# A hybrid RG-LRU and neighbourhood-attention layer: how silu(c) is spread, which loads come in halves, where h is split, and when the bias tables and the decay are made

## The chip, the cores and the metric

The kernel runs on one core of one Trainium2 chip. The metric is the device time of one execution in microseconds. Three runs of the kernel before gave 560.02, 560.91 and 561.32 us, so the median is 560.91 us. One more execution was recorded by the hardware profiler; it took 561.25 us.

## The reference, cut to what matters

One encoder layer, batch 1, 512 tokens, 1024 channels, all in float32. `c` is one vector of 1024 numbers. It gives a scale and a shift for each channel, the normalised input is multiplied and shifted by them to `h`, and `h` goes through one wide projection whose eight parts feed a recurrent branch and an attention branch.

```python
mod = jax.nn.silu(c) @ w_c[l] + b_c[l]
shift, scl, gate = jnp.split(mod, 3, axis=-1)
h = rms_norm(x, g_pre[l]) * (1.0 + scl[:, None, :]) + shift[:, None, :]
proj = h @ w_in[l]
xa, za, q, k, v, zb, ga, gb = jnp.split(proj, split_pts, axis=-1)
...
h_fwd = rg_lru(xa, w_r_f[l], b_r_f[l], w_i_f[l], b_i_f[l], lam_f[l], reverse=False)
h_bwd = rg_lru(xa, w_r_b[l], b_r_b[l], w_i_b[l], b_i_b[l], lam_b[l], reverse=True)
y_a = ((h_fwd + h_bwd).astype(x.dtype) * jax.nn.silu(za)) @ w_pa[l]
y_b = (neighbourhood_attention(qh, kh, vh, rpb[l]) * jax.nn.silu(zb)) @ w_pb[l]
merged = jax.nn.sigmoid(ga) * y_a + jax.nn.sigmoid(gb) * y_b
x = x + gate[:, None, :] * (merged @ w_o[l])
return rms_norm(x, g_final)
```

In `rg_lru` each channel has a decay, `exp(-8 r softplus(-lam))`; in the attention `rpb` is a table of 16 heads x 15 x 31 biases that is added to the scores.

## The kernel before, in words

**Arithmetic.** Each large product is computed as three products on TensorE: both factors are split into a high part of reduced precision (fp32r) and a low part, and high x high, high x low and low x high are added in PSUM (`mm3`). ScalarE makes the high part by a cast, VectorE or GpSimd the low part by a subtraction. So most matrices appear in pairs: `hx` and `lx` (x times the scale), `vh` and `vl` (the weights of v), `hh` and `hl` (h), `whi` and `wlo` (weights of a projection).

**The head of the program.** `par` is one array of 128 x 128 parameters; its first eight rows are `c`. The kernel loads those eight rows as `c8`, computes silu(c) times two there, and spreads it over all 128 partitions by eight matmuls with eight rows each (L460): the result is `pair`, two banks of PSUM that hold the 1024 values on every partition. VectorE multiplies each 128 x 1024 block `wc` of the modulation weights with `pair` and sums (L540; for the first scale in two halves, L536). Each such sum is the scale or the shift of 128 channels (`sc`, `shc`). TensorE meanwhile repeats a matmul of ones (`fill`, L513).

**v first.** v is computed from x times the scale, since the row norm can be applied at the end (`vout`). There are eight units of v (two column halves by four row tiles), each a sum over eight steps k of three matmuls: 192 matmuls. Five units go along step by step, as x and the weights arrive; the other three follow when a step is there.

**h.** When the row norms are known they are spread by TensorE (L506) and copied to `rbs`. For each of the eight blocks k, GpSimd multiplies x with `rbs` into an SBUF tile `ht` (L559), ScalarE applies scale and shift in place (L560) and casts the result to `hh` (L405), and VectorE subtracts for `hl` (L408). The projections (`proj`, matmuls into `acc`, 24 for each) need all eight pairs.

**The rest.** Four groups of attention come first, two pairs of heads each: six projections for q, k and z, then scores (`sp`), softmax, transposes (`pt`) and products with v (`pv`). `bias` makes the tables of one pair of heads on GpSimd, six instructions into three tiles `nb` (L685). Then come the recurrent branch, whose decay constants `small` computes by about thirty instructions of 128 x 16 or 128 x 32 on VectorE (L469, L884 to L902), the merge, the output projection and the final norm.

**Order.** `Plan` is a list scheduler that runs on the host when the program is built. Every operation has a rank, an estimated cost, and the tiles it reads and writes; the planner places operation after operation on the engine on which one can start soonest, prefers the lower rank among those that start at about the same time, and so writes the whole instruction stream of each engine. `HEAD` is a table of ranks that replaces the written ones for some 170 operations of the head. Engines execute their streams in order, and all loads are issued by the SP queue in the order of its stream. `lock=True` tells the planner that a VectorE operation and GpSimd keep each other out. PSUM has eight banks; `LIMITS` bounds how many a class of tiles may hold.

Of the kernel before, what the change touches and what calls it, by code (L numbers as in the profile page):

```python
# [1292 lines left out]
```

## Time and profile before

| | |
|---|---|
| median of three runs | 560.91 us (560.02 to 561.32) |
| profiled execution | 561.25 us, of which the span from the first to the last instruction is 559.3 us |
| TensorE matmul busy | 546.6 us, 98% of the span, 2725 records |
| VectorE, ScalarE, GpSimd busy | 410.5, 329.7 and 127.9 us |
| mean granted TensorE clock | 0.993 |
| moved by DMA | 89.37 MB, mean 160 GB/s; about 410 GB/s in the first 50 us |
| chain that ended last | TensorE 92%, VectorE 5%, DMA 2% |

The 1.95 us between the profiled time and the span lie before the first and behind the last instruction. A row of the groups names a line, an engine, an operation and its tiles, then its count, the busy time and the mean duration of one; behind the next bar stands the time that the engine sat idle just before. A row of the timeline begins with the start of the first instruction and the time from there to the end of the last one that it merges; the idle time before it stands at its end in brackets, with what ended it. Matmuls overlap: a row of one 128x512 matmul reads 0.39 us, though the next one starts about 0.23 us later. A 128x128 matmul in float32 leaves two records.

### The profile page before, as it was taken

The page shows a single profiled execution, that of the slowest core. Times are in us where ns is not written, and L with a number is a line of the kernel's source. Part 1 is how long each engine was busy: PE and PEld are TensorE (multiplying, and loading weights), DVE is VectorE, ACT ScalarE, POOL GpSimd, SP SyncE. Part 2 cuts the span into 40 slices and gives each one's busy share as a digit, 9 for nine tenths or more (in the row PEclk, how much of TensorE's full clock was granted, in tenths as well). Part 3 has the DMA queues.
Part 4 walks back from the last instruction along what each step waited for, and adds up shares of the span by engine and source line. Part 5 has one row for each costly group of instructions (what it writes and reads, how often), then busy time and mean ns, then how long its engine had stood idle before and what let it go on. Part 6 is the DMA issues. An engine that isn't in the chain of part 4 may idle for free.

```text
span 559.3 us, 7626 instructions
## 1 busy us (share of the span) xinstructions
PE 546.6 (98%) x2725; PEld 455.1 (81%) x2725; DVE 410.5 (73%) x715; ACT 329.7 (59%) x575; POOL 127.9 (23%) x114
## 2 busy tenths in 40 slices
PE   8899979999999999999999999999999999999995
PEld 8688768888888888888887888788788888888885
DVE  4978994787787688898458958876967973469523
ACT  4576732763773673675996994996698242223243
POOL 0638865456556540000000000000000000000220
PEclk8999989999999999999999999999999999999999
DMA  8999890544544545125145044221329422380002
GB/s 345 408 410 404 320 361 17 150 150 175 147 161 185 134 152 208 39 95 190 43 132 184 0 151 133 75 102 52 110 86 364 145 83 76 138 313 1 1 38 113
DMA packets 31837, 89.37 MB, mean 160 GB/s; under 512 B 4784, under 2 KB 5944, under 8 KB 31800
## 3 DMA queue, kind: packets, MB, share of 16 engines
q1 hardware_dynamic: 31496, 88.56, 45.0%
q8 instruction: 21, 0.34, 0.3%
q10 hardware_dynamic: 304, 0.33, 0.2%
q14 instruction: 16, 0.13, 0.1%
HBM read 82.42 MB, written 6.46 MB: 159 GB/s over the span
## 4 chain that ended last, share of the span: by engine, by line
PE 92%; DVE 5%; DMA 2%; issue 1%; ACT 1%; ACTq 0%
PE acc L411 77%; PE hx L411 5%; PE pv L411 3%; PE pt L811 2%; PE sp L411 2%; PE gt L411 2%; DVE hhl L408 1%; DMA wraw<-in_w_in_dram 1%; DVE wc L540 1%; DVE vhl L408 1%; DVE xhl L550 1%; DMA c<-in_par_dram 1%; PE pair L460 0%; PE mi L506 0%; DVE va L629 0%
## 5 line engine op out<-in xcount | busy, mean ns | idle before, releaser
L411 PE MATMUL acc<-hhl,whi 128*128 128x512 f32 x784 | 244.4, 392 | 3.1 <-DVE hhl L408 3.1
L411 PEld LDWEIGHTS acc<-hhl,whi 128*128 128x128 f32 x784 | 146.8, 189 | 34.2 <-DVE hhl L408 4.3
L411 PE MATMUL acc<-hhl,wlo 128*128 128x512 f32 x392 | 153.3, 391 | 0.0
L411 PEld LDWEIGHTS acc<-hhl,wlo 128*128 128x128 f32 x392 | 73.9, 189 | 15.6
L1158 POOL TENSOR_TENSOR yo<-yo,gfin 128x512 f32<-128x512 f32 x6 | 8.1, 1358 | 338.6 <-ACT xr L1155 338.6
L405 ACT CAST whi<-wraw 128x1024 fp32r<-128x1024 f32 x72 | 74.1, 1044 | 1.0 <-PE acc L411 0.8
L408 POOL TENSOR_TENSOR wlo<-wraw,whi 128x1024 fp32r<-128x1024 f32 x23 | 56.5, 2462 | 62.7 <-ACT whi L405 32.8
L408 DVE TENSOR_TENSOR wlo<-wraw,whi 128x1024 fp32r<-128x1024 f32 x49 | 59.2, 1219 | 3.1 <-ACT whi L405 2.8
L411 PE MATMUL acc<-woh,mhl 128*128 128x512 f32 (+1 forms) x144 | 40.4, 365 | 0.0
L411 PE MATMUL acc<-yahl,whi 128*128 128x512 f32 x128 | 39.4, 389 | 0.0
L411 PE MATMUL acc<-ybhl,whi 128*128 128x512 f32 x128 | 39.4, 389 | 0.0
L1043 DVE SCALAR_TENSOR_TENSOR gm<-gm,acc 128x512 f32<-128x512 f32 x16 | 11.0, 687 | 33.0 <-PE acc L411 33.0
L800 ACT ACTIVATE p<-p,mn 128x192 f32<-128x192 f32 (+1 forms) x64 | 30.4, 477 | 6.7 <-DVE mn L793 6.6
L685 POOL TENSOR_TENSOR nb<-msk,braw 128x192 f32<-128x192 f32 (+1 forms) x48 | 34.1, 745 | 0.0
L793 DVE CUSTOM_DVE_ANT_0 p<-sp,nb 128x192 f32<-128x192 f32 (+1 forms) x64 | 30.8, 604 | 0.3
L411 PEld LDWEIGHTS acc<-woh,mhl 128*128 128x128 f32 x144 | 26.1, 189 | 4.4
L949 DVE SCALAR_TENSOR_TENSOR xc<-acc,prm,xc 128x511 f32<-128x511 f32 (+1 forms) x24 | 18.0, 750 | 14.8 <-ACT xc L942 14.1
L411 PEld LDWEIGHTS acc<-ybhl,whi 128*128 128x128 f32 x128 | 24.0, 188 | 5.0
L411 PEld LDWEIGHTS acc<-yahl,whi 128*128 128x128 f32 x128 | 24.0, 188 | 5.0
L411 PE MATMUL acc<-wol,mhl 128*128 128x512 f32 (+1 forms) x72 | 26.3, 365 | 0.0
L411 PE MATMUL hx<-vhl,xhl 128*128 128x512 f32 x96 | 24.8, 399 | 1.4 <-DVE vhl L408 1.4
L411 PE MATMUL acc<-ybhl,wlo 128*128 128x512 f32 x64 | 24.9, 389 | 0.0
(186 smaller groups left out, 990.9 us busy)
## 6 DMA issues: line engine op xcount, KB each, us to landing
wraw<-in_w_in_dram SPq DMA_DIRECT2D x56, 512.0 KB
wc<-in_w_m_dram SPq DMA_DIRECT2D x24, 512.0 KB
vt<-vscr SPq DMA_DIRECT2D x20, 256.0 KB
wv<-in_w_v_dram SPq DMA_DIRECT2D x8, 512.0 KB
vscr<-va SPq DMA_DIRECT2D x8, 512.0 KB
wvt<-in_w_vt_dram SPq DMA_DIRECT2D x8, 512.0 KB
wraw<-in_w_pb_dram SPq DMA_DIRECT2D x8, 512.0 KB
wraw<-in_w_pa_dram SPq DMA_DIRECT2D x8, 512.0 KB
```

Source lines behind the costliest of these rows:

```text
L405: return lambda e: nc.scalar.copy(o(), i()) if e == "ACT" else nc.vector.tensor_copy(o(), i())
L408: return lambda e: ENGINE[e].tensor_tensor(o(), a(), b().bitcast(F32), op=ALU.subtract)
L411: nc.tensor.matmul(o, a, b, start=first, stop=last)
L540: op("DVE", dve(1024) + 0.08, lambda e: nc.vector.tensor_tensor_reduce(out=t.ap, in0=t.ap, in1=pair, scale=g, scalar=b, op0=ALU.mult, op1= ...
L550: op("DVE", dve(512) + 0.06, lambda e: nc.vector.scalar_tensor_tensor(lx[k].ap, xk(), scs[k].ap, hx[k].ap.bitcast(F32), op0=ALU.mult, op1= ...
L685: nc.gpsimd.tensor_tensor(o, mv, view, op=ALU.subtract)
L793: nc.vector.tensor_tensor_reduce(out=o, in0=v(spv(h, e)[:, :nk]), in1=v(nb[:, h, :nk]), scale=1.0, scalar=3e38, op0=ALU.add, op1=ALU.min, ...
L800: nc.scalar.activation(pv2(i), pv2(i), AF.Exp, bias=mn.ap[:, c:c + 1], scale=-1.0, accum_out=sm.ap[:, 4 * h + b:4 * h + b + 1])
L811: nc.tensor.transpose(ptp.ap[:, j * P:(j + 1) * P], pt_.ap[:, j * P:(j + 1) * P], ident.ap)
L949: nc.vector.scalar_tensor_tensor(a, b, wcol, a, op0=ALU.mult, op1=ALU.add)
L1043: op("DVE", dve(512), lambda e: nc.vector.scalar_tensor_tensor(t.ap, t.ap, 1.0, o.ap, op0=ALU.add, op1=ALU.mult), n - 1.9, r=[o], rw=[t], ...
L1158: op(("DVE", "POOL"), (dve(w), pool_(w)), lambda e: ENGINE[e].tensor_tensor(y(), y(), gfin[n].ap[:, gs], op=ALU.mult), rank + 0.1, r=[gfin ...
```

## The change

The matmul that spreads silu(c) now contracts over 128 rows: `c8` is cleared by VectorE and its first eight rows are written. There is one load of `par` in place of two. The spread is computed twice: first into two plain banks `cb0`, of which the first scale reads each half by itself, and then into `pair` for all others. The first block of x and the first block of v's weights come in two loads of 256 KB each. The sixth unit of v goes along with the five, one step behind. h is written by ScalarE into a PSUM tile (class `hs`, two banks at most), from which the high part is cast and the low part subtracted. The bias tables of the first pair of heads are asked for behind the tenth projection and later, and the decay behind the thirtieth. The table `HEAD` has new numbers throughout, which moves loads and instructions of the head.

```diff
-LIMITS = {"cb": 2, "hx": 6, "acc": 3, "sp": 8, "pt": 2, "pv": 2, "mi": 2, "hd": 3, "gt": 8}
+LIMITS = {"cb": 2, "hx": 6, "acc": 3, "sp": 8, "pt": 2, "pv": 2, "mi": 2, "hs": 2, "gt": 8}
...
-    "rn": -24.5555, "sq3": -24.3814, "rd": -24.3812, "sq1": -24.3808, "rbs": -23.8168, "sq0": -23.8167,
+    "rb": -26.6107, "rd": -25.5608, "rv": -25.1307, "rn": -25.1305, "sq0": -24.9778, "sq2": -24.9777,
...
-    tan8, c8 = const("tan8", [8, P]), const("c8", [8, P])
+    tan8, c8 = const("tan8", [8, P]), const("c8", [P, P])
-    op("ACT", 0.45, lambda e: nc.scalar.dma_start(c8.ap, par[:8, :]), -41, w=[c8], late=2.6, name="c8")
-    op("ACT", 0.45, lambda e: nc.scalar.dma_start(par_sb.ap, par), -40, w=[par_sb], late=3.3, name="par")
+    clear = op("DVE", 0.25, lambda e: nc.vector.memset(c8.ap, 0.0), -40, w=[c8])
+    op("ACT", 0.45, lambda e: nc.scalar.dma_start(par_sb.ap, par), -40, w=[par_sb], late=2.1)
...
-    cbs = [B("cb") for _ in range(2)]
+    def spread_c(t, n, rank, name):
+        def f(e):
+            for k in range(4):
+                nc.tensor.matmul(t.ap[:, k * P:(k + 1) * P], ident.ap[:, 4 * n + k:4 * n + k + 1].to_broadcast([P, P]), c8.ap,
+                                 start=True, stop=True)
+        op("PE", 0.9, f, rank, r=[ident, c8], w=[t], name=name)
+    cb0 = [B("mi") for _ in range(2)]
     for n in range(2):
-        def f(e, n=n):
-            for k in range(4):
-                nc.tensor.matmul(cbs[n].ap[:, k * P:(k + 1) * P], ident.ap[:8, 4 * n + k:4 * n + k + 1].to_broadcast([8, P]), c8.ap,
-                                 start=True, stop=True)
-        op("PE", 0.6, f, -21 + n, r=[ident, c8], w=[cbs[n]], name=f"cb{n}")
+        spread_c(cb0[n], n, -21 + 0.1 * n, f"ca{n}")
+    cbs = [pl.tile("cb", lambda i, n=n: bank(i, "cb", n)) for n in range(2)]
+    for n in range(2):
+        spread_c(cbs[n], n, -20.5 + 0.1 * n, f"cb{n}")
...
-    for j in range(4):
+    xs = [xT[0].part(0, S), xT[0].part(S, D)] + [xT[k // 2] for k in range(2, KD)]
+    for j in range(2):
+        load(xs[j], whole(xs[j]), x_t[0, :, j * S:j * S + S], -19.9 + 0.1 * j, 262144, spare=2, name=f"x0{'ab'[j]}")
+    for j in range(1, 4):
         load(xT[j], whole(xT[j]), x_t[j], -19.9 + 0.1 * j, 524288, spare=2, name=f"x{j}")
...
         hh[k], hl[k] = two("hhl") if k else (T("hh", F32R), T("hl", F32R))
-        t = T("ht")
+        t, b = T("ht"), B("hs")
...
-        op("ACT", act(512, 2), lambda e: nc.scalar.activation(t.ap, t.ap, AF.Identity, scale=scs[k].ap, bias=shs[k].ap), k - 1.195,
-           r=[scs[k], shs[k]], rw=[t], name=f"hs{k}")
-        op("ACT", act(512), cast(whole(hh[k]), whole(t)), k - 1.19, r=[t], w=[hh[k]], name=f"hh{k}")
-        op("DVE", dve(512), sub(whole(hl[k]), whole(t), whole(hh[k])), k - 1.18, r=[t, hh[k]], w=[hl[k]], lock=True, wait=1.45, name=f"hl{k}")
+        op("ACT", act(512, 2), lambda e: nc.scalar.activation(b.ap, t.ap, AF.Identity, scale=scs[k].ap, bias=shs[k].ap), k - 1.195,
+           r=[t, scs[k], shs[k]], w=[b], name=f"hs{k}")
+        op("ACT", act(512), cast(whole(hh[k]), whole(b)), k - 1.19, r=[b], w=[hh[k]], name=f"hh{k}")
+        op("DVE", dve(512), sub(whole(hl[k]), whole(b), whole(hh[k])), k - 1.18, r=[b, hh[k]], w=[hl[k]], name=f"hl{k}")
...
+        for n in range(2 * (k == 0)):
+            load(src[n], whole(src[n]), w_v[k, :, z[n]], k - 4.5, 262144, spare=2, name=f"wv0{'ab'[n]}")
...
-    for m, u in enumerate(VU[5:]):
+        vmm(VU[5], k, [0, 1, 2], k + 0.9 if k < KD - 1 else k + 0.5)
+    for m, u in enumerate(VU[6:]):
...
-    small(9, [main[8]])
...
-            nbs.append(bias(pr, n0 + BD * (1 - pr % 2), gate_of(n0, 2) if pr else [main[6]]))
+            if pr:
+                nbs.append(bias(pr, n0 + BD * (1 - pr % 2), gate_of(n0, 2)))
...
+            if not pr:
+                nbs.append(bias(pr, n0 + 4, [main[10]]))
...
+    small(31, [main[30]])
```

Three places show how the instructions move. The first is TensorE at the start of the program (`hx` with `onesc` are the fills, `mi` with `par_sb` is a transpose of the parameters, `c` with `ident` is the spread of silu(c), and `vhl` with `xhl` is the first matmul of v). Before:

```order
L513 MATMUL hx_129<-onesc 128x128 x8
L441 MATMUL mi_150<-ident,par_sb 128x128
L460 MATMUL pair<-c_79,ident 128x128 x8
L513 MATMUL hx_129<-onesc 128x128 x10
L411 MATMUL hx_194<-vhl_183,xhl_177 128x512
```

And now:

```order
L523 MATMUL hx_128<-onesc 128x128 x4
L441 MATMUL mi_139<-ident,par_sb 128x128
L523 MATMUL hx_128<-onesc 128x128 x2
L460 MATMUL mi_152<-c_79,ident 128x128 x4
L460 MATMUL mi_159<-c_79,ident 128x128 x4
L460 MATMUL pair<-c_79,ident 128x128 x8
L523 MATMUL hx_128<-onesc 128x128 x2
L411 MATMUL hx_194<-vhl_176,xhl_184 128x512
```

Four fills instead of eight stand ahead of the transpose, the spread has sixteen matmuls instead of eight, and two fills instead of ten stand between it and v.

The second place is GpSimd where h is made (`ht` is x times the row norm, `wlo` the low part of a projection's weights, `nb` a bias table, `vt` a cleared half tile). Before:

```order
L559 TENSOR_TENSOR ht_632<-xT_188,rbs_508 128x512
L408 TENSOR_TENSOR wlo_662<-wraw_461,whi_634 128x1024
L685 TENSOR_TENSOR nb_695<-msk,braw_517 128x256 x2
L685 TENSOR_TENSOR nb_716<-msk,braw_517 128x192 x2
L685 TENSOR_TENSOR nb_737<-msk,braw_517 128x192 x2
L708 MEMSET vt_683 64x512
L708 MEMSET vt_697 64x512
L408 TENSOR_TENSOR wlo_777<-wraw_588,whi_699 128x1024
L685 TENSOR_TENSOR nb_802<-msk,braw_651 128x256 x2
L685 TENSOR_TENSOR nb_823<-msk,braw_651 128x192 x2
L685 TENSOR_TENSOR nb_841<-msk,braw_651 128x192 x2
```

And now:

```order
L569 TENSOR_TENSOR ht_701<-xT_178,rbs_525 128x512
L408 TENSOR_TENSOR wlo_715<-wraw_592,whi_698 128x1024
L723 MEMSET vt_692 64x512
L723 MEMSET vt_706 64x512
L408 TENSOR_TENSOR wlo_766<-wraw_613,whi_752 128x1024
L700 TENSOR_TENSOR nb_787<-msk,braw_660 128x256 x2
L700 TENSOR_TENSOR nb_803<-msk,braw_660 128x192 x2
L700 TENSOR_TENSOR nb_816<-msk,braw_660 128x192 x2
L408 TENSOR_TENSOR wlo_826<-wraw_637,whi_773 128x1024
L700 TENSOR_TENSOR nb_842<-msk,braw_668 128x256 x2
L700 TENSOR_TENSOR nb_856<-msk,braw_668 128x192 x2
L700 TENSOR_TENSOR nb_873<-msk,braw_668 128x192 x2
```

The two sets of bias tables stand one `wlo` later each; all of `ht` and one more `wlo` come before them.

The third place is VectorE where the last blocks of h are split (`hhl` is a tile with a high and a low part, `lt` and `hb` belong to the decay). Before:

```order
L712 STREAM_TRANSPOSE sht_721<-shc 128x32
L408 TENSOR_TENSOR hhl_671<-ht_590,hhl_671 128x512
L408 TENSOR_TENSOR hhl_732<-ht_538,hhl_732 128x512
L469 SCALAR_TENSOR_TENSOR lt_84<-prm 128x16
L884 TENSOR_SCALAR hb<-prm 128x32
L890 TENSOR_SCALAR lt_86<-lt_85 128x16
```

And now:

```order
L727 STREAM_TRANSPOSE sht_708<-shc 128x32
L408 TENSOR_TENSOR hhl_720<-hs_690,hhl_720 128x512
L408 TENSOR_TENSOR hhl_723<-hs_710,hhl_723 128x512
L408 TENSOR_TENSOR hhl_746<-hs_739,hhl_746 128x512
L408 TENSOR_TENSOR ql_789<-acc_633,qh_780 128x512
L754 SCALAR_TENSOR_TENSOR kl_795<-acc_656,kh_785 128x512
```

The subtractions read `hs`, a PSUM tile, instead of `ht`, and the decay is gone from here; its instructions now stand in front of the low part of the fourth group's second k.

More of the change, by code (lines that the diff above doesn't have):

```diff
@@ L37 @@
 VP, VG = 4, 3
-LIMITS = {"cb": 2, "hx": 6, "acc": 3, "sp": 8, "pt": 2, "pv": 2, "mi": 2, "hd": 3, "gt": 8}
+LIMITS = {"cb": 2, "hx": 6, "acc": 3, "sp": 8, "pt": 2, "pv": 2, "mi": 2, "hs": 2, "gt": 8}
 BLOCKS = [(0, 24, 8), (8, 32, 0), (24, 32, 0), (40, 24, 0)]
 HEAD = {
[26 rows of a table removed]
-    "decay": 29.4012
[27 rows of a table added]
 }
@@ L374, in layer, with bank @@
     rest, twin, plain = [], [], set()
-    def bank(i, cls):
+    def bank(i, cls, half=0):
         if cls == "cb":
@@ L379, in bank @@
             twin.append(i)
-            return pair[:, 512 * len(twin) - 512:512 * len(twin)]
+            return pair[:, 512 * half:512 * half + 512]
         if i not in twin:
@@ L536, in modulate @@
                 op("DVE", dve(512) + 0.08, lambda e, j=j, z=z: nc.vector.tensor_tensor_reduce(
-                    out=t.ap[:, z], in0=t.ap[:, z], in1=cbs[j].ap, scale=g, scalar=a.ap if j else b, op0=ALU.mult, op1=ALU.add,
-                    accum_out=r.ap if j else a.ap), -0.5, r=[cbs[j], mods, prm] + [a] * j, rw=[t], w=[r if j else a], name=f"mod{k}{m}{j}")
+                    out=t.ap[:, z], in0=t.ap[:, z], in1=cb0[j].ap, scale=g, scalar=a.ap if j else b, op0=ALU.mult, op1=ALU.add,
+                    accum_out=r.ap if j else a.ap), -0.5, r=[cb0[j], mods, prm] + [a] * j, rw=[t], w=[r if j else a], name=f"mod{k}{m}{j}")
             return
@@ L548, in split_x @@
         op("ACT", act(512, 1), lambda e: nc.scalar.activation(hx[k].ap, xk(), AF.Copy, scale=scs[k].ap), k - 1.19,
[L549 removed]
+           r=[xs[k], scs[k]], w=[hx[k]], name=f"hx{k}")
         op("DVE", dve(512) + 0.06, lambda e: nc.vector.scalar_tensor_tensor(
             lx[k].ap, xk(), scs[k].ap, hx[k].ap.bitcast(F32), op0=ALU.mult, op1=ALU.subtract), k - 1.18,
[L552 removed]
+           r=[xs[k], hx[k], scs[k]], w=[lx[k]], lock=True, name=f"lx{k}")
@@ L554, in make_h @@
     def make_h(k):
         hh[k], hl[k] = two("hhl") if k else (T("hh", F32R), T("hl", F32R))
-        t = T("ht")
+        t, b = T("ht"), B("hs")
         xk = lambda: xT[k // 2].ap[:, k % 2 * 512:k % 2 * 512 + 512]
-        op("POOL", pool_(512), lambda e: nc.gpsimd.tensor_tensor(t.ap, xk(), rbs.ap, op=ALU.mult), k - 1.2, r=[xT[k // 2], rbs], w=[t], name=f"ht{k}")
-        op("ACT", act(512, 2), lambda e: nc.scalar.activation(t.ap, t.ap, AF.Identity, scale=scs[k].ap, bias=shs[k].ap), k - 1.195,
-           r=[scs[k], shs[k]], rw=[t], name=f"hs{k}")
@@ L562, in make_h @@
-        op("ACT", act(512), cast(whole(hh[k]), whole(t)), k - 1.19, r=[t], w=[hh[k]], name=f"hh{k}")
-        op("DVE", dve(512), sub(whole(hl[k]), whole(t), whole(hh[k])), k - 1.18, r=[t, hh[k]], w=[hl[k]], lock=True, wait=1.45, name=f"hl{k}")
+        op("POOL", pool_(512), lambda e: nc.gpsimd.tensor_tensor(t.ap, xk(), rbs.ap, op=ALU.mult), k - 1.2, r=[xs[k], rbs], w=[t], name=f"ht{k}")
+        op("ACT", act(512, 2), lambda e: nc.scalar.activation(b.ap, t.ap, AF.Identity, scale=scs[k].ap, bias=shs[k].ap), k - 1.195,
+           r=[t, scs[k], shs[k]], w=[b], name=f"hs{k}")
@@ L565, in split_v @@
+        op("ACT", act(512), cast(whole(hh[k]), whole(b)), k - 1.19, r=[b], w=[hh[k]], name=f"hh{k}")
+        op("DVE", dve(512), sub(whole(hl[k]), whole(b), whole(hh[k])), k - 1.18, r=[b, hh[k]], w=[hl[k]], name=f"hl{k}")
     def split_v(k):
         t, z = W("wv"), (slice(0, S), slice(S, D))
-        load(t, whole(t), w_v[k], k - 4.5, 524288, spare=2, name=f"wv{k}")
+        src = [t] * 2 if k else [t.part(0, S), t.part(S, D)]
+        if k:
+            load(t, whole(t), w_v[k], k - 4.5, 524288, spare=2, name=f"wv{k}")
@@ L571, in split_v @@
             vh[k, n], vl[k, n] = (hi, whole(hi)), (lo, whole(lo))
-            op("ACT", act(512), lambda e, hi=hi, n=n: nc.scalar.copy(hi.ap, t.ap[:, z[n]]), k - 1.1, r=[t], w=[hi], name=f"vh{k}{n}")
-            op(*(("POOL", pool_(512)) if k and n else (("DVE", "POOL"), (dve(512), pool_(512)))), sub(whole(lo), lambda n=n: t.ap[:, z[n]], whole(hi)), k - 1.09, r=[t, hi],
+            op("ACT", act(512), lambda e, hi=hi, n=n: nc.scalar.copy(hi.ap, t.ap[:, z[n]]), k - 1.1, r=[src[n]], w=[hi], name=f"vh{k}{n}")
+            op(*(("POOL", pool_(512)) if k and n else (("DVE", "POOL"), (dve(512), pool_(512)))), sub(whole(lo), lambda n=n: t.ap[:, z[n]], whole(hi)), k - 1.09, r=[src[n], hi],
                w=[lo], lock=True, name=f"vl{k}{n}")
@@ L903, in small @@
         for j in range(0, len(steps), 2):
-            op("DVE", 0.4, lambda e, j=j: [f() for f in steps[j:j + 2]], rank, r=[lt[1], prm], rw=[lt[2]], w=[sp2, sp4],
-               name="decay")
-    small(9, [main[8]])
+            op("DVE", 0.4, lambda e, j=j: [f() for f in steps[j:j + 2]], rank + 8, r=[lt[1], prm], rw=[lt[2]], w=[sp2, sp4],
+               lock=True, name="decay")
     LO_A = ("POOL",)
```

8 lines of the change are left out of this document (3 added, 5 removed), and 51 rows, old and new, of the table HEAD.

## The prediction

> **What bounds the kernel now.** I read the busy times by stage first, then what TensorE waited for, then the timelines of the stages that are not full, and the chain of waits last. The stages here are: up to the first matmul of v, v up to the first projection, the projections up to the first scores, everything up to the last matmul, and the tail. The columns are each engine's busy time and records, the granted clock, DMA.
>
> ```profile
> 0.00:10.98 10.98, 9.27 (x53) 8.91 (x54) 3.51 (x11) 4.92 (x8) 1.02 (x10) 0.89 0.84 325
> 10.98:58.00 47.02, 45.58 (x202) 37.14 (x202) 41.55 (x63) 31.62 (x52) 26.99 (x21) 0.99 1.03 408
> 58.00:96.29 38.29, 35.16 (x147) 27.76 (x145) 29.29 (x47) 15.69 (x22) 28.88 (x27) 0.96 0.65 233
> 96.29:552.90 456.61, 456.57 (x2329) 381.31 (x2328) 333.80 (x589) 276.48 (x493) 70.97 (x57) 1.00 0.37 124
> 552.90:559.30 6.40, 0.00 (x0) 0.00 (x0) 2.31 (x8) 1.02 (x2) 0.00 (x0) 0.90 0.36 140
> PE acc L411 <- DVE hhl L408: 3.1, 1, 3.1
> PE hx L411 <- DVE vhl L408: 1.4, 1, 1.4
> ```
>
> From 96.29 us on, TensorE is busy for 456.57 of 456.61 us at full clock, so that whole part moves with its beginning. Only the first 96 us can be shortened, and there the long waits are one of 3.1 and one of 1.4 us.
>
> The pace comes from the next rows: four 128x512 matmuls from 22.20 to 23.11 us are 0.2275 us each.
>
> ```profile
> 22.20 1.07 PE L411 MATMUL hx<-vhl,xhl 128*128 128x512 f32 x4
> 23.11 0.39 PE L411 MATMUL hx<-vh,xhl 128*128 128x512 f32 x1
> 43.48 1.05 PE L506 MATMUL mi<-ident,rxc 128*128 128x128 f32 x8
> 44.28 0.94 PE L411 MATMUL hx<-vhl,xhl 128*128 128x512 f32 x3
> 69.42 0.39 PE L411 MATMUL acc<-hhl,whi 128*128 128x512 f32 x1
> 72.91 0.50 PE L411 MATMUL acc<-hhl,whi 128*128 128x512 f32 x1 [3.10 <-DVE hhl L408]
> ```
>
> The 192 matmuls of v need 43.68 us and the spread of the norms 0.80 us, 44.48 together; the stage took 47.02, an excess of **2.54 us**. The six projections (144 matmuls) need 32.76 us; their stage took 38.29, an excess of **5.53 us**. Of that, 69.42 to 72.91 less one matmul is 3.26 us.
>
> The clock, in stretches of 3.4 us as it was granted:
>
> ```profile
> 5.03:8.45 3.42, 3.23 (x27) 1.00 1.01 407
> 8.45:11.86 3.41, 3.41 (x17) 0.50 1.03 417
> 22.10:25.51 3.41, 1.97 (x10) 1.00 1.02 407
> 69.70:73.10 3.40, 0.29 (x2) 1.00 1.02 277
> 73.10:76.50 3.40, 3.40 (x9) 0.53 0.99 392
> ```
>
> An almost empty stretch (0.29 us busy) is followed by one at half speed: 3.4 us of matmuls do the work of 1.7, so the wait of 3.26 cost about 1.7 more. But a stretch with 3.23 us busy also led to half speed at 8.45. What was odd in it is the spread of silu(c): eight rows instead of 128. A stretch with 1.97 us of full matmuls kept full speed.
>
> **The change, part by part.** *h from PSUM, tables and decay later.* The cause of the wait of 3.26 us:
>
> ```profile
> 65.96 2.41 POOL L408 TENSOR_TENSOR wlo<-wraw,whi 128x1024 fp32r<-128x1024 f32 x1
> 68.33 3.38 POOL L685 TENSOR_TENSOR nb<-msk,braw 128x256 f32<-128x256 f32 x6
> 66.75 6.11 DVE L408 TENSOR_TENSOR hhl<-ht,hhl 128x512 fp32r<-128x512 f32 x2
> 61.01 0.86 DVE L629 SCALAR_TENSOR_TENSOR va<-hx,rxc,va 128x256 fp32r<-128x256 f32 x2
> 60.49 4.34 POOL L685 TENSOR_TENSOR nb<-msk,braw 128x256 f32<-128x256 f32 x6
> L408 DVE TENSOR_TENSOR hhl<-ht,hhl 128x512 fp32r<-128x512 f32 x6 | 11.2, 1895 | 0.8 <-ACT hhl L405 0.8
> L408 DVE TENSOR_TENSOR ql<-acc,qh 128x512 fp32r<-128x512 f32 x2 | 1.4, 684 | 0.0
> L560 ACT ACTIVATE ht<-ht,shc,sc 128x512 f32<-128x512 f32 x8 | 6.5, 815 | 4.8 <-DVE shc L540 3.7 <-POOL ht L559 1.1
> ```
>
> Two subtractions from SBUF took 6.11 us: they stood until GpSimd had ended a `wlo` and six `nb`. Six of them average 1895 ns. At 61.01 two operations with a PSUM source ran in 0.86 us while GpSimd worked on `nb`: they are not held. `ql`, the same subtraction from PSUM, takes 684 ns. So the eight low parts cost 0.68 each, VectorE gets back 6 x (1.895 - 0.684) = 7.3 us, and the wait goes: the excess of **5.53** is removed, with the half-speed stretch. No row has ScalarE writing to PSUM in this shape; between the copy out of PSUM (0.59 us for `rbs`) and twice the 0.815 of L560, I take 0.815, the same operation. ScalarE is busy for 15.69 of 38.29 us in the stage, which covers 8 x 0.8 more; without that cover it would be 6.5 us. [...]
>
> What is late next? GpSimd now does eight `ht`, five `wlo`, two memsets and twelve `nb` in a row. By these rows (`ht` 10.09 for eight, `wlo` 2.41, memsets 1.10, `nb` 4.34 + 3.38) that is 31 us.
>
> ```profile
> 45.23 10.09 POOL L559 TENSOR_TENSOR ht<-xT,rbs 128x512 f32<-128x512 f32 x8 [0.80 <-ACT rbs L405]
> 64.89 1.10 POOL L708 MEMSET vt<- 64x512 f32 x2
> ```
>
> From about 44 us it ends at 75; the tables are read after the first scores, at about 88. The last `ht` stands behind two `wlo`: 44 + 10.1 + 4.8 = 58.9, and with 0.82, 0.62 and 0.68 us for shift, cast and subtraction h is whole at about 61 to 63. TensorE wants it 54 matmuls into the projections, at about 55 + 12.3 = 67. The margin is 4 us.
>
> The decay's thirty small instructions now stand ahead of the fourth group's second `kl`.
>
> ```profile
> 213.63 0.69 DVE L408 TENSOR_TENSOR ql<-acc,qh 128x512 fp32r<-128x512 f32 x1 [1.24 <-ACT qh L405]
> 220.43 0.69 DVE L739 SCALAR_TENSOR_TENSOR kl<-acc,kh 128x512 fp32r<-128x512 f32 x1
> 224.77 0.36 PE L411 MATMUL sp<-kh,qh 64*128 64x192 f32 x2
> 81.41 0.17 DVE L897 TENSOR_SCALAR lt<-lt 128x16 f32<-128x16 f32 x1
> 81.62 0.17 DVE L896 TENSOR_TENSOR lt<-lt,lt 128x16 f32<-128x16 f32 x1
> ```
>
> At 0.21 us each, 26 of them behind `ql` are 5.5 us; with three small PSUM operations `kl` ends near 221.7 instead of 221.1 on the old scale, 3 us before the scores want it, since other work moved behind it. Cost nothing; 5.5 us without that cover.
>
> *The sixth unit.* With five units a step is 15 x 0.2275 = 3.41 us; its loads (one `wc`, one `wv`, a quarter of a megabyte of x, 1.31 MB at 408 GB/s) need 3.2. With six it is 4.10, so TensorE falls behind the loads and the wait of 1.4 us goes, whichever load or subtraction caused it. Only two units instead of three cover the making of h; the margins above include that. No work is added: **2.54** removed, of which about 0.5 is the half clock at 10.98 to 11.86.
>
> *The start.* The chain now:
>
> ```profile
> 1.52 3.73 PE L513 MATMUL hx<-onesc 128*128 128x128 f32 x16 [1.52 <-POOL onesc L429]
> 4.88 0.31 ACT L435 ACTIVATE tan<-c 8x128 f32<-8x128 f32 x1 [1.58 <-DMA c<-in_par_dram]
> 5.55 2.04 PE L460 MATMUL pair<-c,ident 8*128 8x128 f32 x16 [0.19 <-DVE c L438]
> 7.53 3.80 PE L513 MATMUL hx<-onesc 128*128 128x128 f32 x20
> 7.64 0.81 DVE L536 CUSTOM_DVE_ANT_0 wc<-wc,pair,mods 128x512 f32<-128x512 f32 x1 [1.33 <-PE pair L460]
> 9.34 0.72 ACT L548 ACTIVATE xhl<-xT,sc 128x512 fp32r<-128x512 f32 x1 [2.64 <-DVE sc L536]
> 10.98 1.59 PE L411 MATMUL hx<-vhl,xhl 128*128 128x512 f32 x4
> ```
>
> One load instead of two, issued 0.44 us sooner: the tanh starts between 4.44 and 4.88; I take 4.7, the spread then 5.37. It took 1.98 us for 16 records, 0.124 each. The first half of the scale can start after eight records (6.4 instead of 7.64), the second after sixteen (7.4), and the scaled x is ready near 9.0. But TensorE's stream is in order: 32 records of spread and four of fills are 36 x 0.124 = 4.5 us, so v starts at **9.8**, 1.2 us sooner. The load halves take the weights out of this path (0.64 us less to wait for); they cost nothing while the loads run at 408 GB/s either way. At half clock all this is longer (rival one).
>
> **Sum** against the profiled execution: 561.25 - 1.2 - 2.54 - 5.53 = 551.98. In both stages about 0.6 us of the excess is neither of the named waits nor clock (2.54 - 1.44 - 0.5; 5.53 - 3.26 - 1.7); I leave half of each in place, +0.6: 552.6. The median lies 0.34 below the profiled run, so **552.3 us**.
>
> **Rivals.** *One: the clock.* Only four fills stand ahead of the transpose, 0.233 us a record in the cold (3.73 for 16), so TensorE stands idle from about 3.4 to 4.9. If that stretch counts as idle, half clock lasts to 8.45: 13 records by then, 23 more at 0.124, v at 11.3. Or 128 rows, nearly all zero, count as little as eight did: 25 records by 8.45, eleven at 0.2 (3.80 for 20, mostly in the half clock), v at 10.65 and then 1.2 us at half speed. Either is 1.5 to 1.7 us worse, 554.0. For it: no stretch between 1.3 us of full-row work (5.03, without the spread) and 1.97 tells where the limit lies, and the new first stretch has about 2. Against: 1.97 sufficed to stay warm. [...]
>
> *Two: part of the wait comes back.* One `wlo`, table or h late: GpSimd and VectorE are the fullest after TensorE. Half of 3.26 and a half-speed stretch is 3.3 us, 555.6; the margin of 4 us speaks against it.
>
> *Three, the other side: the two PSUM banks for h.* Each new `hs` waits until the subtraction two blocks back has let go of its bank, ScalarE's stream stands behind it, and VectorE has sums of 1.27 us and pairs of 0.86 in between. If nothing overlaps, a block takes 0.82 + 0.62 + 0.68 + 1.35 + 0.86 = 4.33 us, eight take 34.6 from 45.3, and h is whole at 79.9, 13 us late; with 1.7 of half clock that is 567. It is slower than before once h is over 7 us late. Against: two banks do overlap, and VectorE loses its 7.3 us of standing.
>
> *Four: nothing arrives,* since another wait of the same size appears, 560.5.
>
> **How the numbers follow.** Forecast 52%, rival one 27%, two 14%, three 4%, four 3%. Lower end: the left 0.6 gone and the tanh at 4.44 is 0.9 less, and runs scatter by 0.9 downward: 550.4. Upper end: rival two and as much again of a run's scatter, 556.5. Faster by over 0.2% (1.1 us, about what a measurement of this kernel tells from no change): 94%; within: 2%; slower: 4%.
>
> **What would show it.** First v matmul at 9.8, first projection near 54.5, first scores near 87.6; no wait of TensorE over 0.5 us before the scores; subtractions for `hl` at 0.7 us each; granted clock 1.00 from 5 us on. Wrong would be: half clock in 5.0 to 8.5 or 8.5 to 11.9 (rival one), TensorE waiting for `hhl` or `wlo` (two, three), or a new wait at the fourth group's scores (decay).

## The result, and the profile after

The changed kernel took 554.21 us, the median of four runs (553.97 to 554.99). The kernel before took 560.46 us beside it (median of four, 558.41 to 561.32). The ratio is 0.9896 with a 95% interval of 0.9867 to 0.9926. The forecast was 552.3 us, with a range of 550.4 to 556.5. The profiled execution took 554.22 us, 7.03 less than the profiled execution of the kernel before.

The stages of the changed kernel follow, cut at the same events as the first fence of the prediction: the first matmul of v, the first projection, the first scores, the last matmul.

```profile
0.00:10.50 10.50, 7.96 (x49) 7.67 (x50) 3.67 (x12) 4.92 (x8) 1.01 (x10) 1.00 0.82 289
10.50:55.45 44.95, 44.92 (x204) 36.95 (x203) 35.94 (x59) 30.00 (x49) 26.13 (x20) 1.00 1.03 407
55.45:88.18 32.73, 32.73 (x146) 26.85 (x145) 14.61 (x20) 17.24 (x23) 31.22 (x31) 1.00 0.88 307
88.18:545.71 457.53, 457.53 (x2329) 381.19 (x2328) 337.89 (x617) 275.92 (x494) 70.87 (x57) 1.00 0.37 125
545.71:552.10 6.39, 0.00 (x0) 0.00 (x0) 2.31 (x8) 1.02 (x2) 0.00 (x0) 0.85 0.33 125
```

| stage | before | forecast | after |
|---|---|---|---|
| up to the first matmul of v | 10.98 | 9.8 | 10.50 |
| v | 47.02 | 44.8 | 44.95 |
| projections up to the first scores | 38.29 | 33.1 | 32.73 |
| first scores to the last matmul | 456.61 | 456.61 | 457.53 |
| tail | 6.40 | 6.40 | 6.39 |
| profiled time less the span | 1.95 | 1.95 | 2.12 |

The sum of the differences is -0.48 - 2.07 - 5.56 + 0.92 - 0.01 + 0.17 = -7.03. The two waits are gone: what TensorE still waited for, over the whole span, lies ahead of v.

```profile
PE hx L523 <- POOL onesc L429: 1.5, 1, 1.5
PE mi L441 <- DMA par_sb<-in_par_dram: 1.0, 1, 1.0
```

And h is made as forecast. In the groups of the stretch from 40 to 100 us the low parts take 0.686 us each, where six of them averaged 1.895, and ScalarE's write to PSUM takes 0.783, close to the 0.815 that was taken for it:

```profile
L570 ACT ACTIVATE hs<-ht,shc,sc 128x512 f32<-128x512 f32 x8 | 6.3, 783 | 0.7 <-DVE shc L550 0.7
L408 DVE TENSOR_TENSOR hhl<-hs,hhl 128x512 fp32r<-128x512 f32 x7 | 4.7, 686 | 2.1 <-ACT hhl L405 2.1
```

Two rows of the table disagree with the forecast: the start is 0.7 us late, and the part that was to move as a rigid block grew by 0.92.

### The profile page after: what moved, and what is told of

It reads as the page before. It is cut to its first block, busy times and chain, and to the rows that moved or that the text cites. A ratio compares the mean times of both kernels' runs of the same rounds, so it can differ in the third digit from the quotient of the medians.

```text
span 552.1 us, 7620 instructions
## 1 busy us (share of the span) xinstructions
PE 543.1 (98%) x2721; PEld 452.7 (82%) x2721; DVE 394.4 (71%) x713; ACT 329.1 (60%) x575; POOL 129.2 (23%) x117
## 4 chain that ended last, share of the span: by engine, by line
PE 98%; DMA 1%; DVE 0%; ACT 0%; issue 0%
PE acc L411 79%; PE hx L411 8%; PE pv L411 3%; PE gt L411 2%; PE pt L826 2%; PE sp L411 2%; DMA par_sb<-in_par_dram 1%; PE mi L460 0%; PE pair L460 0%; PE hx L523 0%; PE mi L516 0%; DVE yo L1198 0%; PE mi L441 0%; DVE yo L1166 0%; DVE xr L1170 0%; ACT sd L1188 0%
## 5 line engine op out<-in xcount | busy, mean ns | idle before, releaser
L411 PE MATMUL acc<-yahl,wlo 128*128 128x512 f32 x64 | 24.9, 389 | 0.0
```

The source lines that it names most:

```text
L411: nc.tensor.matmul(o, a, b, start=first, stop=last)
```

## The experiments

Seven runs undo a part of the change in the changed kernel, two try a part alone in the kernel before, and three add fills or move the decay further. Times are medians; a ratio is against the kernel before, run beside it. Between the groups of runs the kernel before varied between 560.5 and 562.8 us, so small differences are read from the stages of the profiles.

### Making h

**h in SBUF, tables late.**

```diff
-        t, b = T("ht"), B("hs")
+        t = T("ht"); b = t
...
-r=[b, hh[k]], w=[hl[k]], name=f"hl{k}")
+r=[b, hh[k]], w=[hl[k]], lock=True, wait=1.45, name=f"hl{k}")
```

> The changed kernel, only with h again written in place in SBUF, as before (its high part cast and its low part subtracted from there); the bias tables stay late. Theory A (the low parts of h stand behind GpSimd's unbroken work because both their operands are in SBUF): the subtractions average well over 0.69 us again, up to 2.4 each, the length of the wlo they stand behind; the last of them ends between 65 and 68 us against 65.1, where TensorE wants it near 67.7, so a wait of 0 to 1.5 us at most and 554 to 556 us. Rival B (the tables alone held them): with the tables late, they take 0.7 to 0.8 us each, no wait, 554.2. Rival C (the place of h alone decides): the wait of 3.26 and the half-clock stretch come back whole, about 559.

It took 559.01 us (ratio 0.9963, 0.9937 to 0.9988); the projections took 37.09 us instead of 32.73. In the timeline around the longest wait the last low part of h stood for 5.90 us, behind a `wlo` and six `nb`:

```profile
67.37 2.40 POOL L408 TENSOR_TENSOR wlo<-wraw,whi 128x1024 fp32r<-128x1024 f32 x1
67.77 5.90 DVE L408 TENSOR_TENSOR hhl<-ht,hhl 128x512 fp32r<-128x512 f32 x1 [0.39 <-ACT hhl L405]
69.74 3.38 POOL L700 TENSOR_TENSOR nb<-msk,braw 128x256 f32<-128x256 f32 x6
73.72 0.50 PE L411 MATMUL acc<-hhl,whi 128*128 128x512 f32 x1 [1.81 <-DVE hhl L408]
```

Theory A had the mechanism, but far too small: the low part stood for much longer than the one `wlo` (5.90 us against 2.40). Rival B falls, and C has the time: the place of h decides, though the wait came back as several (2.5 us behind low parts of h, 0.3 behind a `wlo`) and without a half-speed stretch; the stage's other 1.4 us are busy time (34.14 us against 32.73). The tables, though asked for late, were what the last block met, since without PSUM the planner's order makes h later.

**Tables early, h in PSUM.**

```diff
-            if pr:
-                nbs.append(bias(pr, n0 + BD * (1 - pr % 2), gate_of(n0, 2)))
+            nbs.append(bias(pr, n0 + BD * (1 - pr % 2), gate_of(n0, 2) if pr else [main[6]]))
...
-            if not pr:
-                nbs.append(bias(pr, n0 + 4, [main[10]]))
```

> The changed kernel, only with the first pair's bias tables asked for early again; h stays in PSUM. Theory A (a subtraction with a PSUM source is not held by GpSimd): the low parts stay at 0.69 us, no wait of TensorE over 0.3 us before the scores, 554.2 within 0.5. Rival B (the tables delay a low part of a weight or a block of h on GpSimd itself, whichever memory h is in): a wait at a wlo or at h, 1 to 5 us more.

554.47 us; the projections took 32.73 us, exactly as in the changed kernel, and the low parts 0.685 each. Theory A holds: with h in PSUM, the place of the tables is worth nothing here.

**Both as before.** The two edits above together.

> The changed kernel with h in SBUF and the tables early, both as before. Theory A: the last three or four low parts of h stand behind a wlo and six tables, about 6 us; h is whole at 68 to 71 where TensorE wants it near 67.7, so a wait of 1 to 3.3 us, and a half-speed stretch of 1.7 if it is near the upper end: 555.5 to 559.2. Rival B (the new order of loads and the sixth unit have already moved h out of the way): no wait, 554.2.

557.78 us (ratio 0.9929, 0.9911 to 0.9947). The projections took 35.00 us, with waits of 0.7 us for a low part of h and 0.4 for a `wlo`; a third, of 0.5, lies in the first scores. The time is within theory A, but the wait for h is shorter than it said. Here a low part ended while the `nb` still went on:

```profile
64.29 3.53 DVE L408 TENSOR_TENSOR hhl<-ht,hhl 128x512 fp32r<-128x512 f32 x3 [0.68 <-ACT hhl L405]
66.15 4.78 POOL L700 TENSOR_TENSOR nb<-msk,braw 128x256 f32<-128x256 f32 x6
68.35 1.10 DVE L408 TENSOR_TENSOR hhl<-ht,hhl 128x512 fp32r<-128x512 f32 x1 [0.52 <-ACT hhl L405]
```

Six `nb` took 4.78 us instead of 3.38, with low parts beside them up to 67.82 and from 68.35 to 69.45. That both edits together cost less than h in SBUF alone fits a loss that hangs on what GpSimd happens to do beside the last low parts; why a low part took 1.10 us here and 5.90 there is open.

**One part alone: h in PSUM in the kernel before.** The same edit to `make_h`, with `"hs": 2` among the limits.

> The kernel before with one part of the change alone: h written to PSUM and split from there (two banks). Theory A (this part alone removes the wait of 3.26 and the half-speed stretch behind it): the subtractions take 0.69 us, the stage from the first projection to the first scores takes 32.8 to 33.5 us instead of 38.29, and the time falls by 4.5 to 5.6 us. Rival B (the bias tables must move too, since they delay a low part of a weight): a wait of 1 to 3 us stays before the scores, the gain is 2 to 4 us. Rival C (two banks serialise the making of h): no gain.

570.45 us, ratio 1.0148 (1.0125 to 1.0172): slower by 7.6 us, where theory A had a gain and the worst of the rivals none. The stage rows for v and for the projections:

```profile
10.84:60.34 49.50, 45.95 (x200) 36.46 (x200) 43.70 (x69) 32.88 (x54) 32.02 (x26) 1.00 1.02 402
60.34:104.97 44.63, 38.16 (x144) 30.33 (x144) 24.64 (x45) 14.39 (x20) 22.84 (x22) 0.85 0.56 178
```

There are three waits. Two, of 2.07 and 1.78 us, are for the high and the low part of the first block: the two banks were passed on slowly, since the subtractions that free them stood among VectorE's sums, and the low part of block 0 came fifth. The third, 4.67 us, is another thing, in the timeline of VectorE, GpSimd and TensorE:

```profile
69.18 6.00 DVE L897 TENSOR_SCALAR lt<-lt 128x16 f32<-128x16 f32 x1
69.45 2.38 POOL L408 TENSOR_TENSOR wlo<-wraw,whi 128x1024 fp32r<-128x1024 f32 x1
71.79 3.36 POOL L685 TENSOR_TENSOR nb<-msk,braw 128x256 f32<-128x256 f32 x6
75.31 0.68 DVE L408 TENSOR_TENSOR hhl<-hs,hhl 128x512 fp32r<-128x512 f32 x1
76.05 0.79 PE L411 MATMUL acc<-hhl,whi 128*128 128x512 f32 x1 [4.67 <-DVE hhl L408]
```

A decay instruction of 128 x 16, which takes 0.17 us elsewhere, stood for 6.00 us, until a `wlo` and six `nb` had ended. The last low part of h, which then took 0.68 us, was queued behind it. So h in PSUM did not pay here, because the decay, which stood beside GpSimd's work in these rows, was ahead of it in VectorE's stream. The changed kernel has the decay 140 us later. The waits brought half speed with them: the granted clock reads 0.85 over the projections, matmuls stood 0.43 us apart from 63.67 to 67.1 us and again from 76.64 on, and TensorE was busy for 38.16 us in the projections, 5.4 more than the changed kernel's 32.73. A run with PSUM and only the decay moved was not made, so how much of the 7.6 us is the decay's and how much the banks' is read from these waits alone.

### v

**The sixth unit behind the others again.**

```diff
-        vmm(VU[5], k, [0, 1, 2], k + 0.9 if k < KD - 1 else k + 0.5)
-    for m, u in enumerate(VU[6:]):
+    for m, u in enumerate(VU[5:]):
```

> The changed kernel with the sixth unit of v behind the others again, so five units go along with the loads. Theory A (a step of five units, 3.41 us, runs into loads of 3.2 us and what is made of them): waits of 1 to 2.5 us within v, 555.2 to 556.7. Rival B (the order of the loads and the halves removed the wait, not the sixth unit): no wait, 554.2. With the sixth unit later, more work covers the making of h, so nothing is lost there in either case.

554.67 us, and no wait in v:

```profile
11.27:55.84 44.57, 44.57 (x203) 37.04 (x202) 35.92 (x59) 29.95 (x49) 26.15 (x20) 1.00 1.03 408
```

The stage needs 44.48. So with the new ranks the excess of 2.54 us is gone without the sixth unit (rival B). v started 0.77 us later than in the changed kernel and took 0.38 less, which gives the small loss.

**The old ranks.** The code of the changed kernel, with the table `HEAD` of the kernel before; names that are new got the rank of what they stand for.

> The changed kernel's code with the ranks of the table as they were (names that are new take the ranks of the loads and spreads that they stand for). The five-unit run had no wait in v, so the sixth unit is not what removed the wait of 1.44 us. Theory A (the new ranks removed it, by which low parts of v's weights go to GpSimd and which to VectorE): the stage from the first matmul of v to the first projection has waits of 1 to 3 us again, 45.5 to 48 instead of 44.9, even with six units; 555 to 557.5. Rival B (the halves of the first loads and the earlier start removed it): no wait in v, 554.2 within 0.5.

556.57 us (ratio 0.9922, 0.9896 to 0.9948). The first projection came 2.8 us later than in the changed kernel. Of that, 1.66 are the start: v started at 12.16, and in this profile TensorE's full pace came at 10.3 us. The other 1.15 are v, which took 46.10 us, with a wait of 0.72 us and some shorter ones. The groups of v's low parts show what the ranks do. In the kernel before, then in the changed kernel, then in this run (each over the stage of v):

```profile
L408 POOL TENSOR_TENSOR vl<-wv,vh 128x512 fp32r<-128x512 f32 x7 | 11.2, 1620 | 18.9 <-ACT vh L572 18.9
L408 DVE TENSOR_TENSOR vhl<-wv,vhl 128x512 fp32r<-128x512 f32 x6 | 7.3, 1230 | 0.0
L408 POOL TENSOR_TENSOR vhl<-wv,vhl 128x512 fp32r<-128x512 f32 x2 | 3.0, 1506 | 0.0
```

```profile
L408 POOL TENSOR_TENSOR vl<-wv,vh 128x512 fp32r<-128x512 f32 x7 | 9.6, 1377 | 8.5 <-ACT vh L586 8.5
L408 POOL TENSOR_TENSOR vhl<-wv,vhl 128x512 fp32r<-128x512 f32 x5 | 6.5, 1307 | 11.9 <-ACT vhl L586 11.9
L408 DVE TENSOR_TENSOR vhl<-wv,vhl 128x512 fp32r<-128x512 f32 x2 | 2.5, 1235 | 1.5 <-ACT vhl L586 1.5
```

```profile
L408 DVE TENSOR_TENSOR vhl<-wv,vhl 128x512 fp32r<-128x512 f32 x6 | 7.3, 1231 | 0.0
L408 POOL TENSOR_TENSOR vhl<-wv,vhl 128x512 fp32r<-128x512 f32 x2 | 3.0, 1510 | 0.0
```

With the old ranks VectorE makes six of them with two operands in SBUF, at 1.23 us each, 7.3 us in all; with the new ones GpSimd takes three more, and VectorE spends 2.5 us there. As at h, they stand beside GpSimd's work, one stage earlier; with GpSimd idle such a part took 0.68 us (at 10.76 us in the kernel before). In the kernel before, the rows at its wait in v are these:

```profile
22.84 1.72 POOL L408 TENSOR_TENSOR vhl<-wv,vhl 128x512 fp32r<-128x512 f32 x1
23.36 1.75 DVE L408 TENSOR_TENSOR vhl<-wv,vhl 128x512 fp32r<-128x512 f32 x1
25.17 2.14 PE L411 MATMUL hx<-vhl,xhl 128*128 128x512 f32 x8 [1.44 <-DVE vhl L408]
```

With the old ranks the wait is back at the same pair of rows (1.73 on GpSimd, 1.77 on VectorE). Its size is not: 0.72 us instead of 1.44, and what is left of that difference may be the sixth unit's or the halves'. The table of ranks also sets the order of the loads, and no run has the one without the other.

**The first loads whole.** One load of 512 KB each for the first blocks of x and of v's weights.

> The changed kernel with the first blocks of x and of v's weights in one load of 512 KB each. Theory A (v is held in its middle at about 33 us, so a start up to 1 us later costs nothing there): v starts at 10.9 to 12, the first projection at 55.4 to 56.3, 554.2 to 555.1. Rival B (halves matter, the bytes ahead of v decide): v starts 0.6 to 1.3 us later and all of it arrives at the end: 555 to 555.6.

554.78 us; v started at 11.43, took 44.66 us, and the first projection came at 56.09, 0.64 later than in the changed kernel. These numbers lie in theory A's ranges, but its reason fails: v was not held in its middle, and the later start arrived whole, as rival B says (the changed kernel's own v took 0.29 more). How much of the later start is the halves' and how much a later change of pace (it came between 7.4 and 10.3 us in other runs with the same fills, as the last part shows), one profile can't tell.

### The start

**Seven fills ahead of the transpose instead of four.** The first `fill` issues four matmuls instead of one.

> The changed kernel with seven fills instead of four ahead of the transpose, so that TensorE works without a gap from 1.5 us on. In the profiles so far the matmuls run at 0.213 us a record at first and at 0.112 from some point on: 5.65 us in the kernel before (no gap), 7.44, 8.73, 8.40, 8.50 and 9.05 in the changed kernel and its variants (gap from 3.4 to 4.6). Theory A (the gap resets the warm-up, which takes one to two stretches of 3.41 us from the start of unbroken work): the change of pace comes between 4.9 and 8.3 us instead of 7.2 to 10.6, v starts between 9.4 and 10.5, and the end is up to 1 us sooner if nothing else holds v: 553.3 to 554.2. Rival B (v is held by its loads anyway): v starts sooner and waits in its middle, 554.2 within 0.3. Rival C (128 rows that are nearly all zero do not count): the pace changes no sooner than 7.4.

553.71 us (553.61 to 554.37). The profiled execution is the slowest of the six. In it the pace changed at 4.5 us, v started at 9.40, and then it waited 1.32 us at 33.7. The rows around the wait:

```profile
30.46 1.35 POOL L408 TENSOR_TENSOR vhl<-wv,vhl 128x512 fp32r<-128x512 f32 x1 [0.88 <-ACT vhl L586]
31.77 1.28 POOL L408 TENSOR_TENSOR vl<-wv,vh 128x512 fp32r<-128x512 f32 x1
31.83 1.77 DVE L560 SCALAR_TENSOR_TENSOR xhl<-xT,sc,xhl 128x512 fp32r<-128x512 f32 x1
33.66 1.21 PE L411 MATMUL hx<-vhl,xhl 128*128 128x512 f32 x4 [1.32 <-DVE xhl L560]
```

Rival B in this profile: v starts 1.1 us sooner and the first projection comes at 55.60, where it came at 55.45. What holds v is not a load here: a low part of x, again with two operands in SBUF, took 1.77 us, where the first one of the kernel before took 0.75 with GpSimd idle, and it ended only behind GpSimd's pause at 33.05. The median is another matter: 553.71 lies in theory A's range and below rival B's, so in other executions some of the earlier start may have arrived.

The other profiles show where that hold begins. v that starts at 10.47, 10.92, 10.98, 11.27 and 11.43 us (both fills and decay, tables early, decay later, five units, whole loads) takes 44.54 to 44.66 us each time, so from there on a later start arrives whole. The changed kernel itself, from 10.50, takes 44.95: TensorE meets the same low part of x, which took 1.77 us there too, about 0.2 us too early.

**Eight rows again.**

```diff
-    tan8, c8 = const("tan8", [8, P]), const("c8", [P, P])
+    tan8, c8 = const("tan8", [8, P]), const("c8", [8, P])
...
-ident.ap[:, 4 * n + k:4 * n + k + 1].to_broadcast([P, P]), c8.ap,
+ident.ap[:8, 4 * n + k:4 * n + k + 1].to_broadcast([8, P]), c8.ap,
```

> The changed kernel with the spread of silu(c) over eight rows again, still twice. Theory A (few rows do not count for the clock): from 5.7 us on 32 records of eight rows are as good as idle, so the pace stays at 0.213 through the spread, v starts at 12.0 to 12.8 and its first microseconds run at half speed: the first projection at 56.0 to 58.5 instead of 55.4, 554.7 to 557.3. Rival B (rows do not matter, only busy time): as the changed kernel, first projection at 55.4 to 55.9, 554.2 to 554.7.

558.99 us (ratio 0.9965, 0.9946 to 0.9984), 4.8 more than the changed kernel and 1.7 above theory A's range. The spread in TensorE's timeline, and the first matmuls of v:

```profile
6.31 3.78 PE L460 MATMUL mi<-c,ident 8*128 8x128 f32 x16
9.89 3.62 PE L460 MATMUL pair<-c,ident 8*128 8x128 f32 x16
14.31 2.06 PE L411 MATMUL hx<-vhl,xhl 128*128 128x512 f32 x4
```

TensorE was busy without a gap from 6.3 us, and still all 32 records (0.22 us each) and the first six matmuls of v ran at half pace, to 17.0 us. In the changed kernel, where the same 32 records are on 128 rows, of which 120 are zero, the pace changed among the first of them, at 7.4 us. So between these two runs the rows counted, and that most of them hold zeros did not. Theory A in its cause, too small in its size: v started at 14.3 where it said 12.0 to 12.8, since the fills ran at half pace too, and lost 1.4 us more in its first matmuls.

**One part alone: 128 rows in the kernel before.**

> The kernel before with one part of the change alone: the spread of silu(c) over 128 rows, in the same eight matmuls. Theory A (full rows count for the clock, and v is held in its middle anyway): no half-speed stretch behind 8 us, v starts at 9.9 to 10.4 instead of 10.97, and a longer wait in v takes most of it back: the first projection at 57.2 to 57.9 instead of 57.99, a gain of 0.1 to 0.8 us. Rival B (the start passes through to the end): a gain of 1 to 1.5 us. Rival C (rows do not count): the half-speed stretch stays, no gain.

561.36 us, ratio 0.9982 (0.9965 to 1.0). The half-speed stretch was gone (the clock reads 1.00 from 10.39 to 57.68 us), v started at 10.39, and the first projection came at 57.68, 0.31 sooner: theory A by the profile. The medians can't tell it from rival B, since their interval runs from no gain to 2 us. TensorE waited 0.8 us for a cast of ScalarE ahead of v, which is why v did not start sooner still, and the wait for a low part at 25 us stayed (1.4 us).

### Behind the scores

In the changed kernel TensorE is busy in every row from the first scores on, and yet the part takes 0.92 us more. Instruction by instruction the difference gathers at one place, the gate products of the recurrent branch's first group. They stand in one piece in the kernel before (twelve pairs, at 262.2 us). After the change there are three pieces, and this is the first of them and the second:

```profile
252.95 0.39 PE L411 MATMUL acc<-hhl,wlo 128*128 128x512 f32 x1
253.27 0.50 PE L411 MATMUL gt<-xh,gwh 64*128 64x512 f32 x2
253.60 0.40 PE L411 MATMUL gt<-xl,gwh 64*128 64x512 f32 x2
253.84 0.40 PE L411 MATMUL gt<-xh,gwl 64*128 64x512 f32 x2
254.17 1.22 PE L411 MATMUL pv<-pp,vt 128*128 128x256 f32 x8
255.31 0.50 PE L411 MATMUL gt<-xh,gwh 64*128 64x512 f32 x2
```

Within a piece a pair starts 0.23 us after the one ahead, as matmuls of 128 rows do. But the first pair starts 0.32 after the last matmul of 128 rows (252.95 to 253.27) and the second 0.33 after the first; and the matmul behind the piece starts 0.33 after the last pair. With its successor, by the same pattern 0.1 late, that is four times 0.1, so a visit costs about 0.4 us, and there are two more.

**The decay ranked later**, past the fourth group's second `kl`; the planner then puts the gate products together again. Eight of the decay's instructions still stand ahead of that `kl`, and the rest behind it, in pieces up to 231 us.

```diff
-"hh4": 16.6705, "decay": 26.9995
+"hh4": 16.6705, "decay": 33
```

> The changed kernel with the decay's twenty-six small instructions ranked some units later, past the fourth group's second kl, so that the planner puts the first group's four gate products in one piece again (one visit to 64-row matmuls instead of three). Theory A (every change between matmuls of 128 and 64 rows costs about 0.2 us, so two more visits cost 0.85): from the first scores to the last matmul 456.6 instead of 457.5, 553.3 to 553.5. Rival B (the 0.9 us lies elsewhere, spread over the whole part): 457.3 or more, 554.2. Rival C (the decay stands in the way of the first recurrence there): a wait of TensorE behind 250 us, over 554.5.

553.83 us, with v and the projections as in the changed kernel (first projection at 55.52, first scores at 88.25), and the rest

```profile
88.25:544.93 456.68, 456.68 (x2329) 381.49 (x2328) 337.38 (x617) 276.37 (x494) 70.88 (x57) 1.00 0.38 125
```

which is 0.85 less than 457.53. Theory A by this stage, though the median is 0.3 above its range. The other profiles repeat it: with the decay where the change put it, the part takes 457.4 to 457.7 us in seven more of them (458.3 in the run with its wait of 0.5 in the scores), and with the decay later also 456.73 in the last run below. So the decay's move did cost 0.85 us, by way of the planner and not of VectorE's time. The rows of the gates put the price at about 0.2 us for each change between matmuls of 128 and of 64 rows.

**Both: seven fills and the decay later.**

> The changed kernel with seven fills ahead of the transpose and the decay's instructions ranked later, both together. Theory A (the gate products in one piece are worth 0.85 us; the earlier start is lost again in the middle of v): v starts at 9.4 to 10.5, first projection at 55.4 to 55.6, from the first scores to the last matmul 456.6; 553.2 to 553.8. Rival B (the earlier start also steadies the time, since v no longer starts after 11 in some executions): a median up to 0.5 below the run with the decay alone, 553.3. Rival C (neither adds to the other): 553.8.

553.39 us (553.33 to 553.47), ratio 0.9845 (0.9825 to 0.9866). All four runs are below those of the kernel before, and below all of the changed kernel's, which were made in another group. Its stages:

```profile
10.47:55.02 44.55, 44.55 (x203) 37.03 (x202) 35.89 (x59) 30.09 (x49) 26.14 (x20) 1.00 1.03 408
55.02:87.75 32.73, 32.73 (x145) 26.84 (x143) 14.61 (x20) 17.24 (x23) 31.26 (x31) 1.00 0.90 309
87.75:544.48 456.73, 456.73 (x2329) 381.34 (x2328) 337.35 (x617) 276.51 (x494) 70.92 (x57) 1.00 0.38 125
```

The first two are within 0.1 us of what the matmuls need (44.48 and 32.76), and the third within 0.15 of the kernel before. Theory A holds for the time, but not by its reason at the start: in this profile the seven fills changed nothing there. The full pace came at 7.4 us, as in the changed kernel, and v started at 10.47. The first projection, at 55.02, came 0.4 us sooner than theory A had it.

## Why the prediction was right, and where its steps were wrong

The direction and the range held, 554.21 in 550.4 to 556.5. The time lies 1.9 us above the forecast and beside rival one's 554.0, but at most 0.7 of it for that rival's reason.

**The wait at h: right in its cause and its size.** The term of 5.53 was removed as 5.56, none of it was left, and undoing the PSUM tile brought back 4.4 us of it. What the text gave the tables and the decay was misplaced. The tables' move is worth nothing with h in PSUM (32.73 us either way). The decay's was costed only at its new place; at its old one it stood in VectorE's stream ahead of the last low part of h, and in the run with PSUM alone TensorE waited 4.67 us for that part. Rival three, at 4%, had the price right for the kernel before with this part alone (567 forecast, 570 measured), but two banks were only a part of its mechanism. In the changed kernel h was whole at 65.1 us, not at 61 to 63, where TensorE wanted it near 67.7: a margin of 2.6 us, not 4.

**v: nearly the right size for a wrong reason, which is luck.** The excess of 2.54 went down to 0.47. The step "With six it is 4.10, so TensorE falls behind the loads and the wait of 1.4 us goes, whichever load or subtraction caused it" failed: with five units the wait stayed away. The row of the wait named the releaser, a low part of v's weights on VectorE, and the groups show that three of these went to GpSimd. DMA was full (share 1.03, 408 GB/s over v in the kernel before), but what TensorE ran into at that wait were held subtractions: the low part that ended it took 1.75 us and the low part of x ahead of it 1.83, where alone such parts take 0.68 and 0.75. The old ranks brought back 1.15 of the 2.07 us; what the rest came from is open.

**The start: the step on TensorE's stream failed.** "36 x 0.124 = 4.5 us" took the pace that the spread had in the kernel before. TensorE's timeline shows that four fills and the first eight records of the spread ran at 0.213 us each (4.88 to 7.44), so the spread began at 5.73 instead of 5.37 and v at 10.50:

```profile
1.51 2.07 PE L523 MATMUL hx<-onesc 128*128 128x128 f32 x8 [1.51 <-POOL onesc L429]
4.61 0.48 PE L441 MATMUL mi<-ident,par_sb 128*128 128x128 f32 x1 [1.02 <-DMA par_sb<-in_par_dram]
5.73 2.78 PE L460 MATMUL mi<-c,ident 128*128 128x128 f32 x16
8.35 1.95 PE L460 MATMUL pair<-c,ident 128*128 128x128 f32 x16
10.50 1.18 PE L411 MATMUL hx<-vhl,xhl 128*128 128x512 f32 x4
```

This looks like the first half of rival one, the gap from 3.6 to 4.6 us, in a milder form, but the runs don't show that the gap is the cause: with seven fills and no gap, the full pace came at 4.5 us in one profile and at 7.4, as here, in the other. The rival's second half, that zero rows count little, is refuted by the run with eight rows (full pace at 17.0 us, against 7.4 with 128). And "granted clock 1.00 from 5 us on" was a poor test: the column reads 1.00 where the records are 0.213 us apart. The step behind it, that the start passes through to the end, held only in part: v that starts at 9.40 ended where v that starts at 10.50 ended, while starts from 10.47 to 11.43 arrived whole.

**The rest: "moves with its beginning" failed by 0.92 us.** The decay was costed at nothing because `kl` had 3 us to spare, and `kl` did end at 213.3, which is 221.4 on the old scale where 221.7 was forecast, with no wait behind it. But a planner that is given one later operation writes another order 40 us on. The prediction weighed the new order at three places and not at the gates.

In sum, 0.7 us at the start, 0.9 at the gates, 0.2 outside the span and 0.15 in v were missed, and 0.35 more was gained at the projections: the 1.6 us between 552.6 and the profiled execution's 554.22.

## What to carry to other kernels

Where a VectorE instruction takes far longer than its twin elsewhere (5.90 us against 0.69 here), look at what GpSimd does at that moment before looking at loads, and look at everything that stands ahead of the late instruction in VectorE's stream: moving the operand to PSUM freed only the instruction itself here (0.68 us, behind one of the decay that stood for 6.00). A stage with two limits can give back what is gained on one (v that started 1.1 us sooner ended 0.15 later), so an earlier start is worth its first projection and not its first matmul. And where a planner writes the order, count the changes between kinds of matmul in the whole stream (about 0.2 us each here), not only near the edit.
